# Seven-product pairs: the four sums are cast and split in two halves, and the products come in another order

## The chip, the core and the metric

The kernel runs on one core of a Trainium2 chip. The metric is the device time of one launch in microseconds (us). The engines are PE (TensorE, matmuls), DVE (VectorE), ACT (ScalarE), POOL (GpSimd) and SP (SyncE, which here only issues DMA transfers).

## The reference

A two-layer encoder trunk for 256 tokens of width 2048. Layer 0 mixes tokens by neighbourhood attention and a gated recurrence, layer 1 by a pooling mixer and grouped attention. Each mixer is followed by a SwiGLU block of hidden width 5632, which is where the change lies:

```python
def swiglu(x, w_gate, w_up, w_down):
    return (jax.nn.silu(x @ w_gate) * (x @ w_up)) @ w_down
...
for layer in range(DEPTH):
    ...
    x = layer_norm(DN_ALPHA * x + y, ln_mix_g[layer], ln_mix_b[layer])
    f = swiglu(x, ffn_w_gate[layer], ffn_w_up[layer], ffn_w_down[layer])
    x = layer_norm(DN_ALPHA * x + f, ln_ffn_g[layer], ln_ffn_b[layer])
```

All data are float32.

## The kernel before

**Precision.** PE multiplies in a rounded 32-bit format (`fp32r`). So each operand is kept as two parts: `hi`, a cast by ACT, and `lo`, the rest, by a subtraction on DVE. The helper `split` issues the two (L127, L128). A product of two such operands takes three matmuls (`mm3`, L292: hi·lo, hi·hi, lo·hi), each 128 x 128 by 128 x 512.

**SwiGLU.** The hidden width is cut in 11 chunks of 512 columns, and the chunks in three phases of 3, 4 and 4. A phase computes gate and up projection of its chunks and then multiplies them into the down projection. The first phase uses a plain form. In the second and third, one call of `unit` makes one chunk: so there are 4 units in a phase, 8 in a layer, 16 in all ("second unit" below is the second of a phase).

A unit runs over 8 pairs of 128-row weight blocks, for gate and up together. A pair is a 2 x 2 block product: two token tiles by gate and up. Most pairs are ordinary: weights come in two loads of 512 KB (`load_half`: tile `raw`, split into `whi` and `wlo`), and take 8 block products. The pairs 5, 6 and 7 (5 and 6 in the last unit of a phase, so 44 in all) are done with seven products (Strassen's scheme in Winograd's form). `load_seven` prepares their weights:

- one load of 1 MB into `rs` (one buffer, L443), which holds four 512-column blocks;
- the cast of the first three blocks on ACT (L444) and their `lo` part on DVE (L448), into entries 0 to 2 of `sh` and `sl`, which have two buffers and seven entries;
- four sums of blocks on DVE into `z` (one buffer): two in one instruction (L445), then one each (L446, L447);
- the split of the four sums into entries 3 to 6 of `sh` and `sl`: one 128 x 2048 cast (L127) and one 128 x 2048 subtraction (L128).

`forms` holds the matching sums of the token side, made once in a phase (tiles `fmh`, `fml`). `SEVEN_ORDER` (L453) names for each product the weight entry, the token form and the PSUM bank.

**Banks and the end of a unit.** The eight PSUM banks form two sides, `aside` and `bside`, four each. A unit gathers in c11, c21, c12, c22 on one side and in the special banks p1, p6, p5, p7 on the other. At its end DVE and ACT combine them (L485 to L499), and the sides change roles: the next unit's c banks are this unit's special banks. PE can begin a bank of the next unit when its last reader has run: p1 is read by L485, p6 by L486, p5 by L487 and L489, p7 by L488.

**What sets the order.** The kernel is written for a scheduler, which chooses the order of instructions on each engine by its own cost estimates and by priorities: the loads and splits of weights are written with priority 400, the end of a unit with 1000. So an edit in `load_seven` may move instructions anywhere in the units. DMAs of weights all go through SP's queue in the order of issue; a load waits for its buffer: `rs` until the last sum (L447) and L448 have read it, `raw` (four buffers) until its `wlo` subtraction has run.

Of the kernel before, what the change touches and what calls it, by code (L numbers as in the profile page):

```python
# [80 lines left out]
def trunk(ctx: ExitStack, tc: tile.TileContext, a, out):  # L81
# [44 lines left out]
    def split(hi, lo, src):  # L126
        nc.scalar.copy(hi, src)  # L127
        return nc.vector.tensor_tensor(lo, src, hi.bitcast(F32), op=sub).ins  # L128
# [304 lines left out]
    def load_seven(sp, src, behind):  # L433

        with ExitStack() as order:
            order.enter_context(tc.high_priority(offset=400))
            if behind:
                order.enter_context(tc.issue_after(behind))
            raw = sp.tile([P, 4, NCH], F32, tag="rs", name="rs", bufs=1)
            hi = sp.tile([P, 7, NCH], F32R, tag="sh", name="sh", bufs=2)  # L440
            lo = sp.tile([P, 7, NCH], F32R, tag="sl", name="sl", bufs=2)
            z = sp.tile([P, 4, NCH], F32, tag="z", name="z", bufs=1)
            last_load[0] = nc.sync.dma_start(raw, src).ins  # L443
            nc.scalar.copy(hi[:, :3], raw[:, :3])  # L444
            nc.vector.tensor_tensor(z[:, :2], raw[:, 0:3:2], raw[:, 3:4].to_broadcast([P, 2, NCH]), op=add)  # L445
            nc.vector.tensor_tensor(z[:, 2], z[:, 0], raw[:, 2], op=add)  # L446
            nc.vector.tensor_tensor(z[:, 3], z[:, 2], raw[:, 1], op=add)  # L447
            nc.vector.tensor_tensor(lo[:, :3], raw[:, :3], hi[:, :3].bitcast(F32), op=sub)  # L448
            split(hi[:, 3:], lo[:, 3:], z)
        return lambda i: (hi[:, i, :], lo[:, i, :])  # L450


    SEVEN_ORDER = ((0, "11", "p1"), (5, "f", "p6"), (3, "e", "p5"), (4, "g", "p7"), (1, "12", "c11"), (2, "h", "c12"), (6, "22", "c21"))  # L453

    def unit(sp, pairs, sevens, w, lhs, forms, yT, opening):

# [2 lines left out]
        left = {n: 4 * (len(pairs) - len(sevens)) // 2 for n in b}  # L459
        for _, _, n in SEVEN_ORDER:  # L460
            left[n] = left.get(n, 0) + len(sevens)

        def product(name, x, wt):
            left[name] -= 1
            mm3(b[name], x, wt, name not in begun, left[name] == 0)
            begun.add(name)

        behind = [low[-n] if opening and n else None for n in BEHIND]
        for p in pairs:
            if p in sevens:  # L470
                if "p1" not in b:
                    b.update((n, side_bank(True)) for n in ("p1", "p6", "p5", "p7"))
                wt = load_seven(sp, w[p], behind.pop(0))
                for i, x, name in SEVEN_ORDER:
                    product(name, forms[p][x], wt(i))
            else:
                for n, ks in ((0, (2 * p, 2 * p + 1)), (1, (2 * p + 1, 2 * p))):
                    hi, lo = load_half(w[p][:, 2 * n : 2 * n + 2])
                    for tok in range(NT):
                        for kk in range(2):  # L480
                            product(f"c{tok + 1}{n + 1}", lhs(tok, ks[kk]), (hi[:, kk, :], lo[:, kk, :]))
                    half_done()
# [658 lines left out]
def build(nc, arrays):  # L1141
    args = {}
    for name, v in arrays.items():
        t = nc.dram_tensor(name, v.shape, mybir.dt.from_np(v.dtype), kind="ExternalInput")
        args[name[3:]] = t.ap()
    out = nc.dram_tensor("out", (T, D), F32, kind="ExternalOutput").ap()
    with tile.TileContext(nc, schedule_with_timeline_sim=True) as tc:
        trunk(tc, args, out)
# [11 lines left out]
```

## Time and profile before

| | |
|---|---|
| median of 3 runs | 2190.99 us (2190.37 to 2191.4) |
| profiled execution: its own time | 2194.07 us |
| profiled execution: its span | 2192.3 us |
| granted PE clock | 0.998 |
| ACT busy | 1051.0 us, 48% |
| POOL busy | 52.1 us, 2% |
| read from memory | 416.78 MB, 191 GB/s over the span |

The profiled execution is one launch, recorded by the hardware; its span is the time from the first to the last recorded instruction, and its own time is a little above. A row of an engine's timeline has the start in us, the duration, the engine, the line, the operation, output and inputs by their names, and the shape; in brackets behind it the idle time before it and what ended that. In the view of DMA issues the last number is the time from issue to landing.

### The profile page before, as it was taken

Reading aid. Unit: us, or ns where it says so; the run is one execution under the profiler, and the core shown is the slowest. Engines: PE = TensorE matmul, PEld = TensorE weight load, DVE = VectorE, ACT = ScalarE, POOL = GpSimd, SP = SyncE. Lnnn points to the kernel's source line nnn. Section 1 sums busy time; section 2 is a strip of 40 time slices with the busy share of each in tenths; the row PEclk is TensorE's granted clock in tenths of the full one; section 3 lists DMA queues with packets and bytes.
Section 4 is the critical chain, followed back from the end, with each engine's and each line's share of the span. In section 5 each row is a group of like instructions: output and inputs, shape, how many; then the busy total and the mean of one; then the engine's idle time right before and its main releaser. Section 6 shows DMA issues by size and latency. Waiting matters only on the chain.

```text
span 2192.3 us, 26626 instructions
## 1 busy us (share of the span) xinstructions
PE 2172.9 (99%) x10048; PEld 1804.1 (82%) x10048; DVE 1558.2 (71%) x1954; ACT 1051.0 (48%) x1278; POOL 52.1 (2%) x51
## 2 busy tenths in 40 slices
PE   9999999999999999999999999999999999999997
PEld 7888888888888888888888888888888888888886
DVE  6886688567537787577876776666367896768865
ACT  6445544546425454444545554455344554445442
POOL 0000001000000000000000300000000000000000
PEclk9999999999999999999999999999999999999999
DMA  8555536684636555565548553747456555655573
GB/s 296 164 164 174 173 126 192 200 286 138 232 123 225 185 204 191 188 232 182 196 158 302 172 183 106 238 147 254 142 185 235 182 179 192 223 174 192 175 247 117
DMA packets 112850, 420.64 MB, mean 192 GB/s; under 512 B 13776, under 2 KB 16848, under 8 KB 105808
## 3 DMA queue, kind: packets, MB, share of 16 engines
q1 hardware_dynamic: 112720, 418.93, 57.5%
q8 instruction: 79, 1.29, 0.2%
q14 instruction: 51, 0.42, 0.1%
HBM read 416.78 MB, written 2.10 MB: 191 GB/s over the span
## 4 chain that ended last, share of the span: by engine, by line
PE 91%; DVE 4%; DMA 3%; issue 1%; ACT 1%; SPq 0%; DVEq 0%; ACTq 0%
PE acc L292 42%; PE bside L292 20%; PE aside L292 18%; PE mx L292 6%; DMA rs<-in_gu 2%; PE mx L729 1%; PE tr L124 1%; DVE wlo L128 1%; DMA raw<-in_gu 1%; DVE sl L448 1%; DVE sl L128 0%; PE mx L775 0%; PE aside L124 0%; PE bside L124 0%; PE mx L985 0%
## 5 line engine op out<-in xcount | busy, mean ns | idle before, releaser
L128 DVE TENSOR_TENSOR wlo<-raw,whi 128x1024 fp32r<-128x1024 f32 (+1 forms) x673 | 817.2, 1224 | 435.2 <-ACT whi L127 424.6
L127 ACT CAST whi<-raw 128x1024 fp32r<-128x1024 f32 (+1 forms) x673 | 703.9, 1052 | 817.5 <-PE acc L292 263.5
L292 PE MATMUL acc<-whi,xTl 128*128 128x512 f32 x864 | 342.8, 397 | 4.8 <-ACT whi L127 4.8
L292 PE MATMUL acc<-whi,xTh 128*128 128x512 f32 x864 | 339.8, 393 | 0.0
L292 PE MATMUL acc<-wlo,xTh 128*128 128x512 f32 x864 | 337.6, 393 | 0.1
L292 PE MATMUL acc<-whi,yTl 128*128 128x512 f32 x512 | 200.6, 392 | 0.1
L292 PE MATMUL acc<-whi,yTh 128*128 128x512 f32 x512 | 199.6, 390 | 0.0
L292 PE MATMUL acc<-wlo,yTh 128*128 128x512 f32 x512 | 197.7, 390 | 0.0
L292 PEld LDWEIGHTS acc<-whi,xTl 128*128 128x128 f32 x864 | 162.9, 189 | 37.0 <-ACT whi L127 5.5
L292 PEld LDWEIGHTS acc<-wlo,xTh 128*128 128x128 f32 x864 | 162.7, 188 | 33.6 <-DVE wlo L128 0.9
L292 PEld LDWEIGHTS acc<-whi,xTh 128*128 128x128 f32 x864 | 163.1, 189 | 31.1
L292 PE MATMUL aside<-whi,xTl 128*128 128x512 f32 x336 | 131.5, 391 | 0.4
L292 PE MATMUL bside<-whi,xTl 128*128 128x512 f32 x336 | 131.4, 391 | 0.3
L292 PE MATMUL aside<-whi,xTh 128*128 128x512 f32 x336 | 131.0, 390 | 0.0
L292 PE MATMUL bside<-whi,xTh 128*128 128x512 f32 x336 | 131.0, 390 | 0.0
L292 PE MATMUL bside<-wlo,xTh 128*128 128x512 f32 x336 | 128.1, 390 | 0.0
L292 PE MATMUL aside<-wlo,xTh 128*128 128x512 f32 x336 | 128.1, 390 | 0.0
L292 PEld LDWEIGHTS acc<-wlo,yTh 128*128 128x128 f32 x512 | 96.1, 188 | 20.5 <-DVE wlo L128 0.5
L292 PEld LDWEIGHTS acc<-whi,yTl 128*128 128x128 f32 x512 | 96.2, 188 | 19.7 <-DVE yTl L991 0.3
L292 PEld LDWEIGHTS acc<-whi,yTh 128*128 128x128 f32 x512 | 96.2, 188 | 19.4
L128 DVE TENSOR_TENSOR sl<-z,sh 128x2048 fp32r<-128x2048 f32 x44 | 100.7, 2289 | 6.7 <-ACT sh L127 6.1
L444 ACT CAST sh<-rs 128x1536 fp32r<-128x1536 f32 x44 | 65.3, 1483 | 76.3 <-DMA rs<-in_gu 35.8
(266 smaller groups left out, 3447.6 us busy)
## 6 DMA issues: line engine op xcount, KB each, us to landing
raw<-in_gu SPq DMA_DIRECT2D x264, 512.0 KB, 4.7
raw<-in_down SPq DMA_DIRECT2D x176, 512.0 KB, 3.9
raw<-in_ab_in SPq DMA_DIRECT2D x127, 512.0 KB, 4.2
rs<-in_gu SPq DMA_DIRECT2D x44, 1024.0 KB, 5.7
raw<-in_cd_in SPq DMA_DIRECT2D x40, 512.0 KB, 4.3
raw<-in_ab_out SPq DMA_DIRECT2D x32, 512.0 KB, 4.5
raw<-in_cd_out SPq DMA_DIRECT2D x32, 512.0 KB, 4.3
bias<-in_na_bias SPq DMA_DIRECT2D x32, 64.0 KB, 4.2
```

What stands on the lines that cost most here:

```text
L124: return nc.tensor.transpose(o, src, eye)
L127: nc.scalar.copy(hi, src)
L128: return nc.vector.tensor_tensor(lo, src, hi.bitcast(F32), op=sub).ins
L292: ins = nc.tensor.matmul(o, lhs[a], rhs[b], start=start and n == 0, stop=stop and n == 2)
L444: nc.scalar.copy(hi[:, :3], raw[:, :3])
L448: nc.vector.tensor_tensor(lo[:, :3], raw[:, :3], hi[:, :3].bitcast(F32), op=sub)
L729: nc.tensor.matmul(m[:, 2 * h + s, :], kk[:, h, s * P : (s + 1) * P], qq[:, h, r * P : (r + 1) * P], start=True, stop=True,)
```

## The change

In `load_seven` the split of the four sums is done in two halves: first the sums 0 and 1 (entries 3 and 4), then the sums 2 and 3 (entries 5 and 6). Each half is a 128 x 1024 cast and a 128 x 1024 subtraction. And in `SEVEN_ORDER` the products of the entries 3 and 4 now come ahead of that of entry 5.

```diff
@@ -446,11 +446,12 @@
             nc.vector.tensor_tensor(z[:, 2], z[:, 0], raw[:, 2], op=add)
             nc.vector.tensor_tensor(z[:, 3], z[:, 2], raw[:, 1], op=add)
             nc.vector.tensor_tensor(lo[:, :3], raw[:, :3], hi[:, :3].bitcast(F32), op=sub)
-            split(hi[:, 3:], lo[:, 3:], z)
+            for s in (slice(0, 2), slice(2, 4)):
+                split(hi[:, 3:][:, s], lo[:, 3:][:, s], z[:, s])
         return lambda i: (hi[:, i, :], lo[:, i, :])
 
 
-    SEVEN_ORDER = ((0, "11", "p1"), (5, "f", "p6"), (3, "e", "p5"), (4, "g", "p7"), (1, "12", "c11"), (2, "h", "c12"), (6, "22", "c21"))
+    SEVEN_ORDER = ((0, "11", "p1"), (3, "e", "p5"), (4, "g", "p7"), (5, "f", "p6"), (1, "12", "c11"), (2, "h", "c12"), (6, "22", "c21"))
```

There are 44 instructions more on ACT and 44 more on DVE; PE has the same number of matmuls. From L450 on, all line numbers of the new kernel are one higher: the first read of p6 is L486 before and L487 after. The scheduler also sets a different order within the second and third phases of both layers. Three places of it:

At the end of a second unit, DVE (`g` and `u` are the tiles of the unit's end, `sl` and `wlo` the `lo` parts of weights). Before:

```order
L445 TENSOR_TENSOR z<-rs 128x1024
L128 TENSOR_TENSOR wlo<-raw,whi 128x1024
L446 TENSOR_TENSOR z<-z,rs 128x512
L448 TENSOR_TENSOR sl<-rs,sh 128x1536
L447 TENSOR_TENSOR z<-z,rs 128x512
L128 TENSOR_TENSOR wlo<-raw,whi 128x1024
L486 TENSOR_TENSOR g_6585<-g_6584,bside 128x512
L487 TENSOR_TENSOR u_6586<-g_6585,bside 128x512
L490 TENSOR_TENSOR g_6584<-g_6584,aside 128x512
L128 TENSOR_TENSOR sl<-z,sh 128x2048
```

And after:

```order
L445 TENSOR_TENSOR z<-rs 128x1024
L128 TENSOR_TENSOR wlo<-raw,whi 128x1024
L446 TENSOR_TENSOR z<-z,rs 128x512
L448 TENSOR_TENSOR sl<-rs,sh 128x1536
L128 TENSOR_TENSOR sl<-z,sh 128x1024
L447 TENSOR_TENSOR z<-z,rs 128x512
L128 TENSOR_TENSOR wlo<-raw,whi 128x1024
L487 TENSOR_TENSOR g_6597<-g_6596,bside 128x512
L128 TENSOR_TENSOR sl<-z,sh 128x1024
L488 TENSOR_TENSOR u_6598<-g_6597,bside 128x512
```

The first half of the split has moved ahead of the last sum and of the first read of p6; the second half stands right behind that read, where the whole split came two instructions later.

At the end of a third unit, DVE. Before:

```order
L486 TENSOR_TENSOR g_6905<-g_6904,aside 128x512
L487 TENSOR_TENSOR u_6906<-g_6905,aside 128x512
L490 TENSOR_TENSOR g_6904<-g_6904,bside 128x512
L128 TENSOR_TENSOR sl<-z,sh 128x2048
L488 TENSOR_TENSOR g_6905<-g_6905,aside 128x512
L492 TENSOR_TENSOR u_6906<-bside,u_6906 128x512
L445 TENSOR_TENSOR z<-rs 128x1024
```

And after:

```order
L487 TENSOR_TENSOR g_6923<-g_6922,aside 128x512
L128 TENSOR_TENSOR sl<-z,sh 128x1024 x2
L488 TENSOR_TENSOR u_6924<-g_6923,aside 128x512
L491 TENSOR_TENSOR g_6922<-g_6922,bside 128x512
L445 TENSOR_TENSOR z<-rs 128x1024
L489 TENSOR_TENSOR g_6923<-g_6923,aside 128x512
```

Both halves come ahead of the reads of p5, and the first sums of the next pair (L445, which waits for that pair's load) ahead of the read of p7 (L489).

At the same place PE, just after the new unit's first seven-product pair. Before:

```order
L292 MATMUL aside_6924<-sh_7018,xTh1_3821 128x512
L292 MATMUL aside_6924<-sl_7019,xTh1_3821 128x512
L292 MATMUL aside_6925<-whi_6946,xTl0_3822 128x512
L292 MATMUL aside_6925<-whi_6946,xTh0_3820 128x512
L292 MATMUL aside_6925<-wlo_6947,xTh0_3820 128x512
```

And after, where `whi_7071` is a raw pair that comes later in the unit:

```order
L292 MATMUL aside_6942<-sh_7036,xTh1_3821 128x512
L292 MATMUL aside_6942<-sl_7037,xTh1_3821 128x512
L292 MATMUL aside_6941<-whi_7071,xTl0_3822 128x512
L292 MATMUL aside_6941<-whi_7071,xTh0_3820 128x512
L292 MATMUL aside_6942<-whi_7071,xTl1_3823 128x512
L292 MATMUL aside_6942<-whi_7071,xTh1_3821 128x512
L292 MATMUL aside_6943<-whi_6964,xTl0_3822 128x512
```

Four matmuls on the banks already open now come ahead of the next bank. Their weights are cast on ACT directly behind the cast of the next pair's `rs` load (L444).

## The prediction

> **What bounds the kernel now.** The first view is the page's own head, the busy time of each engine with its share of the span.
>
> ```profile
> PE 2172.9 (99%) x10048; PEld 1804.1 (82%) x10048; DVE 1558.2 (71%) x1954; ACT 1051.0 (48%) x1278; POOL 52.1 (2%) x51
> ```
>
> PE is busy for 99% of the span, and the diff leaves its work alone: the same products with the same shapes. So the change can only act through moments in which PE stands still or starts late. The waits of PE and the chain give how many there are and how fast PE goes when nothing holds it.
>
> ```profile
> PE acc L292 <- ACT whi L127: 4.8, 1, 4.8
> PE mx L292 <- DVE ptl L128: 1.2, 1, 1.2
> 734.44 2.72 PE aside L292 x12
> ```
>
> The two largest waits (total, times, longest) are 4.8 and 1.2 us, on the banks `acc` and `mx` of other stages. But 12 matmuls in 2.72 us are one per 0.227 us, and against that pace small losses can be read that the waits do not list. They lie at the end of a 512-column unit, where the four PSUM banks of the special products must be read by VectorE before the next unit's matmuls may overwrite them. PE at the end of the second unit of layer 0's second phase, and then of the third unit of layer 1's:
>
> ```profile
> 799.85 0.40 PE L292 MATMUL bside<-whi,xTl 128*128 128x512 f32 x1
> 802.80 0.39 PE L292 MATMUL bside<-sh,xTh 128*128 128x512 f32 x1
> 803.29 0.50 PE L292 MATMUL bside<-sl,xTh 128*128 128x512 f32 x1
> 803.89 0.50 PE L292 MATMUL bside<-whi,xTl 128*128 128x512 f32 x1
> 804.23 0.39 PE L292 MATMUL bside<-whi,xTh 128*128 128x512 f32 x1
> 1796.39 0.50 PE L292 MATMUL aside<-sl,xTh 128*128 128x512 f32 x1
> 1796.98 0.50 PE L292 MATMUL aside<-whi,xTl 128*128 128x512 f32 x1
> 1797.32 0.40 PE L292 MATMUL aside<-whi,xTh 128*128 128x512 f32 x1
> ```
>
> At 802.80 the next start is due 0.227 later, at 803.03, and comes at 803.29: 0.26 lost. The one after it is 0.37 late, the next 0.11: 0.74 us at this end. At 1796 it is 0.36 and 0.11: 0.47 us. Four units (the second of each of four phases) end like the first, two like the other, so all that shorter chains on VectorE could give back is 4 x 0.74 + 2 x 0.47 = 3.9 us, 0.18%. A measurement of this kernel tells about 0.2% from no change, 4.4 us, so the ceiling of the gain lies below what would count as faster.
>
> What those ends wait for is a VectorE chain that begins with the landing of an `rs` load and then runs without a hole. The chain of waits gives the load, VectorE's timeline the rest:
>
> ```profile
> 785.03 7.55 DMA rs<-in_gu
> 792.68 1.23 DVE L445 TENSOR_TENSOR z<-rs 128x1024 f32<-128x1024 f32 x1 [5.33 <-DMA rs<-in_gu]
> 793.83 1.22 DVE L128 TENSOR_TENSOR wlo<-raw,whi 128x1024 fp32r<-128x1024 f32 x1
> 794.96 0.68 DVE L446 TENSOR_TENSOR z<-z,rs 128x512 f32<-128x512 f32 x1
> 795.56 1.75 DVE L448 TENSOR_TENSOR sl<-rs,sh 128x1536 fp32r<-128x1536 f32 x1
> 797.23 0.68 DVE L447 TENSOR_TENSOR z<-z,rs 128x512 f32<-128x512 f32 x1
> 797.83 1.22 DVE L128 TENSOR_TENSOR wlo<-raw,whi 128x1024 fp32r<-128x1024 f32 x1
> 798.97 0.68 DVE L486 TENSOR_TENSOR g<-g,bside 128x512 f32<-128x512 f32 x1
> 799.75 0.69 DVE L487 TENSOR_TENSOR u<-g,bside 128x512 f32<-128x512 f32 x1
> 800.36 0.68 DVE L490 TENSOR_TENSOR g<-g,aside 128x512 f32<-128x512 f32 x1
> 800.95 2.28 DVE L128 TENSOR_TENSOR sl<-z,sh 128x2048 fp32r<-128x2048 f32 x1
> 803.16 0.68 DVE L488 TENSOR_TENSOR g<-g,bside 128x512 f32<-128x512 f32 x1
> ```
>
> From 792.68 to 803.84 VectorE has no free moment. L486 frees p6's bank, L488 the bank that PE takes at 803.89, and the large `sl` subtraction stands between them.
>
> **The split itself.** Prices from the costliest groups and from the tile view of `sh`:
>
> ```profile
> L128 DVE TENSOR_TENSOR sl<-z,sh 128x2048 fp32r<-128x2048 f32 x44 | 100.7, 2289 | 6.7 <-ACT sh L127 6.1
> L128 DVE TENSOR_TENSOR wlo<-raw,whi 128x1024 fp32r<-128x1024 f32 (+1 forms) x673 | 817.2, 1224 | 435.2 <-ACT whi L127 424.6
> L127 ACT CAST whi<-raw 128x1024 fp32r<-128x1024 f32 (+1 forms) x673 | 703.9, 1052 | 817.5 <-PE acc L292 263.5
> L127 ACT CAST sh<-z x44: 1907/1913/1921, 694.7 to 2066.0; 128x2048 fp32r<-128x2048 f32 x44
> ```
>
> A half has the shape of a `wlo` subtraction: 2 x 1.224 - 2.289 = +0.16 us busy per pair on VectorE, 44 times 7 us; on ScalarE 2 x 1.052 - 1.913 = +0.19, 8.4 us. In a back-to-back chain a 1024-wide one takes 1.14 from start to start (797.83 to 798.97) and the large one 2.21 (800.95 to 803.16), so the split lengthens a chain by 0.07 us. Nearly all of it lies beside PE, since VectorE is busy for 71% and ScalarE for 48%; where that cover is gone, at the six ends, the order on VectorE decides, below.
>
> The Trainium skill (VectorE: DVE Perf Modes, section "The DRAIN you can't avoid") says that the next instruction does not start until the pipe is empty. The rows here start each instruction some 0.08 us before the end of the one ahead, so by that rule each half would cost its whole 1.22 us in a chain, and the sum below would be 4 x 0.08 = 0.3 us higher; the rows decide.
>
> **Second units (four ends).** In the new order on VectorE the first `sl` half stands right behind L448 and ahead of L447, `wlo` and the first read of a special bank; the second half right behind that read. ScalarE's half is there by then: the first two sums are done at 793.9, and the cast takes 1.05. Nothing earlier in the chain moves, so with the start-to-start times of the rows: first half 797.23 to 798.37, L447 to 798.97, `wlo` to 800.11, then L486's work, whose end comes 0.68 later, and PE follows 0.06 behind (803.84 to 803.89): 800.85. PE wants that bank at 799.85. So 1.00 us is lost there, where nothing was lost. In exchange the second half and the other three reads end at about 803.9, and PE, now 15 matmuls later (15 x 0.227 = 3.41), reaches the next bank at 804.26 without a wait. Against 803.89 this is **+0.36 us** at each of four ends: one wait takes the place of two, and is longer. The new product order moves p6's product two places back within a pair, 6 matmuls or 1.4 us; the first read of p6 comes when VectorE gets to it, not when PE is done (PE was in the new unit's banks before 799.85), so that stays hidden, and neither costs nor gives.
>
> **Third units.** In layer 1 both halves come ahead of L487, and the sums of the *next* pair ahead of L488: one 1.14 for the sums more ahead of L488's release. PE's order there changes as well: behind the last product of the new unit's first seven-pair come four matmuls of a raw pair, whose cast stands on ScalarE behind the cast of the next `rs` load. The rows of layer 1, then of layer 0:
>
> ```profile
> 1795.91 1.48 ACT L444 CAST sh<-rs 128x1536 fp32r<-128x1536 f32 x1 [1.11 <-PE aside L292]
> 1797.29 1.99 ACT L127 CAST whi<-raw 128x1024 fp32r<-128x1024 f32 x2
> 844.51 0.68 DVE L488 TENSOR_TENSOR g<-g,aside 128x512 f32<-128x512 f32 x1
> 845.54 2.00 ACT L127 CAST whi<-raw 128x1024 fp32r<-128x1024 f32 x2
> 846.47 0.39 PE L292 MATMUL aside<-whi,xTl 128*128 128x512 f32 x1
> ```
>
> The first of the two casts ends at 1797.29 + 1.05 = 1798.34, so PE goes on at 1798.38 and not at 1796.98: **+1.40 us** in each phase of layer 1, in which the second unit's 0.36 is already contained (the chain hangs on a load's landing, not on PE). In layer 0 L488 has ended at 845.19, 1.28 us before PE asks; the cast ends at 846.59 and PE is there at 846.47: +0.1, beside the 0.36 of the second unit.
>
> First units and last units have 2 us and more between the last read and PE's need by the same reckoning, so the extra 0.07 and the moved half stay hidden. At a phase's opening one raw load falls behind an `rs` load on SP's queue; the raw load has about 3 us to spare, so nothing.
>
> Sum so far: 2 x (0.36 + 0.1) + 2 x 1.40 = **+3.7 us**.
>
> **The loads.** An `rs` load of 1 MB takes the longer, the shorter the time since the raw loads ahead of it were issued. Issues of SP, and the landing times:
>
> ```profile
> 824.55 2.12 SPq L168 DMA_DIRECT2D raw<-in_gu  x2
> 830.25 0.33 SPq L443 DMA_DIRECT2D rs<-in_gu  x1
> rs<-in_gu SPq DMA_DIRECT2D x1, 1024.0 KB, 4.7
> 1775.40 2.07 SPq L168 DMA_DIRECT2D raw<-in_gu  x2
> 1780.12 6.57 DMA rs<-in_gu
> 783.12 0.33 SPq L168 DMA_DIRECT2D raw<-in_gu  x1
> DMA to landing us min/median/max: 4.6/5.7/8.8
> ```
>
> The third row answers for the load of 830.25. With 3.58 us between the last raw issue's end and the `rs` issue it lands in 4.7; with 2.65 in 6.57; with 1.58 (783.45 to 785.03) in 7.55. Now the `rs` load after a second unit waits for L447, which the half ahead of it delays by 1.14, and VectorE's raw subtractions behind that pair's sums free their buffers some 0.7 to 1.3 later (an estimate from the same chain). The `rs` load of the third unit keeps its time, since PE releases its `sh` buffer. In layer 0 the gap falls from 3.58 to about 2.9 and the load grows by 1.4; in layer 1 from 2.65 to about 1.7 and it grows by 0.8. Both third-unit chains hang on that landing, so it counts in full once the slack is gone: 2 x 1.4 + 2 x 0.8 = 4.4, less some 0.8 where layer 0's unused wait absorbs it: **+3.6 us**. Bounds: nothing at all (the raw issues do not move), and the slowest landing, 8.8, at both layer 1 ends and 6.57 at both of layer 0: 2 x 2.2 + 2 x 1.9 = 8.2.
>
> The Trainium skill (DMA: Bandwidth & Descriptors, section "Queues, rings and completion order") says that each engine consumes a queue's descriptors in ring order; the three landings agree, since the later load waits out what is left of the earlier ones. By a queue without order the 3.6 would be zero.
>
> Total: 3.7 + 3.6 = +7.3 us on the profiled execution's 2194.07, 2201.4. The median of the runs stands 3.1 below that execution, so **2198 us** is forecast.
>
> **Rivals.**
> - *The loads keep their times* (raw issues are held by something other than VectorE): only +3.7, 2194.7, within 0.2%. For it: between 1.58 and 2.65 the landing changes by 1 us only. Against: the step to 4.7.
> - *Not slower: the early half shortens the chain.* If the `rs` load of the second units lands in 4.7 instead of 7.55, the whole chain begins 2.85 earlier, all six ends are free of waits, and the 3.9 us come back: 2187.1. It decides from a landing 1.0 us shorter on, since then the bank is read by 799.85. For it: with the first half written early, the `sl` buffer is complete sooner for PE. Against: that load is issued when L448 of the pair before is done, at 785.03, and no instruction ahead of that moves.
> - *No effect:* the added waits take the place of waits of the same size; within 1 us of 2191.
> - *Both layers meet the worst landings, and the next pair's sums block VectorE ahead of L488* until an `rs` load lands: 3.7 + 8.2 = +11.9, 2202.9.
>
> **How the numbers follow.** Forecast, with its own range of 2196 to 2201: 0.48. Loads as before, 2194.7: 0.25, of which a fifth lies past the 0.2% line of 2195.4. Chain shortened, 2187.1: 0.10, of which half passes the line of 2186.6. No effect: 0.06. Worst landings: 0.11. Slower: 0.48 + 0.05 + 0.11 = 0.64; same: 0.20 + 0.05 + 0.06 = 0.31; faster 0.05. The range from 2193 to 2203 leaves out the shortened chain and the case of no effect, 0.16.
>
> **What would show it.** PE's waits in the second units: one of about 1.0 us at the first bank of the new unit, with L487 (new numbering) as the releaser, and none later. Third units of layer 1: a gap of 1.6 us ahead of a matmul on `whi`, released by ScalarE's cast. The landing of the third units' `rs` loads: over 6 us in layer 0. VectorE busy 7 us more, ScalarE 8.4. The forecast is wrong if PE enters the new unit at 799.85 without a wait, or if the landings shrink.

## Result and the profile after

The changed kernel's median is 2197.91 us (2194.78 to 2202.66, 11 runs), that of the kernel before beside it 2192.51 (2190.37 to 2196.02): the ratio is 1.0022 with a 95% interval of 1.0014 to 1.0030, or +4.8 us (3.1 to 6.6); the two medians are 5.4 us apart. A later comparison, on another occasion, gave 1.0019 (1.0010 to 1.0028). So it is slower, as forecast in sign, and by two thirds of the forecast +7.3 us in size. The profiled execution took 2195.99 us, 1.9 more than that of before, so it shows less of the loss than the median does; why is the subject of what follows.

The page's head and PE's waits of the changed kernel (L numbers from L450 on are one higher than before):

```profile
span 2194.1 us, 26706 instructions
PE 2171.2 (99%) x10048; PEld 1803.8 (82%) x10048; DVE 1559.9 (71%) x1998; ACT 1054.7 (48%) x1322; POOL 55.5 (3%) x51
```

```profile
PE acc L292 <- ACT whi L127: 5.4, 3, 4.8
PE aside L292 <- ACT whi L127: 2.1, 1, 2.1
PE bside L292 <- ACT whi L127: 1.6, 1, 1.6
PE aside L292 <- DVE g L487: 0.6, 2, 0.4
PE bside L292 <- ACT g L486: 0.5, 1, 0.5
```

The second and third rows are new: PE waits, in the banks of the SwiGLU units, for a cast of ScalarE. Both lie at third units of layer 0. SP, ScalarE and PE at the first of them:

```profile
829.38 0.33 SPq L443 DMA_DIRECT2D rs<-in_gu  x1
840.44 0.33 SPq L443 DMA_DIRECT2D rs<-in_gu  x1
845.74 1.47 ACT L444 CAST sh<-rs 128x1536 fp32r<-128x1536 f32 x1 [4.27 <-PE aside L292]
847.12 1.04 ACT L127 CAST whi<-raw 128x1024 fp32r<-128x1024 f32 x1
845.76 0.39 PE L292 MATMUL aside<-sl,xTh 128*128 128x512 f32 x1
848.21 0.50 PE L292 MATMUL aside<-whi,xTl 128*128 128x512 f32 x1 [2.06 <-ACT whi L127]
```

PE is ready at 845.99 and starts at 848.21, 0.05 after the end of the cast of `whi`. That cast stands behind the cast of the next pair's `rs` load, which was issued at 840.44, landed at 845.36 and was cast from 845.74 on. (The bracket names PE for that wait. The instruction waits for a DMA and for a matmul that ended before 843; a wait for several is put down to the last event that the profile sees.) On ScalarE this cast stood behind that of the load before the change, too (844.16 and 845.54 in the profile of before). What is new is PE's order, which needs it ahead of the next bank. The load of 840.44 waits in its turn for the sums of the pair before it, whose load left at 829.38. So two loads in a row lie on the path, and the slower of the two is the first: 6.7 us, where the one before the change took 4.7.

In layer 1 the same place loses almost nothing, because there the first load landed in 5.0:

```profile
rs<-in_gu SPq DMA_DIRECT2D x1, 1024.0 KB, 5.0
1799.45 0.39 PE L292 MATMUL aside<-sl,xTh 128*128 128x512 f32 x1
1799.98 0.50 PE L292 MATMUL aside<-whi,xTl 128*128 128x512 f32 x1
```

That is 0.30 lost, and 0.37 before the change. Last, the second units. VectorE's chain, PE at the new unit's first bank, and the landing of the load that starts the chain:

```profile
rs<-in_gu SPq DMA_DIRECT2D x1, 1024.0 KB, 6.7
791.68 1.22 DVE L445 TENSOR_TENSOR z<-rs 128x1024 f32<-128x1024 f32 x1 [4.51 <-DMA rs<-in_gu]
796.23 1.22 DVE L128 TENSOR_TENSOR sl<-z,sh 128x1024 fp32r<-128x1024 f32 x1
797.36 0.69 DVE L447 TENSOR_TENSOR z<-z,rs 128x512 f32<-128x512 f32 x1
797.97 1.22 DVE L128 TENSOR_TENSOR wlo<-raw,whi 128x1024 fp32r<-128x1024 f32 x1
799.10 0.68 DVE L487 TENSOR_TENSOR g<-g,bside 128x512 f32<-128x512 f32 x1
799.50 0.39 PE L292 MATMUL bside<-sl,xTh 128*128 128x512 f32 x1
799.84 0.50 PE L292 MATMUL bside<-whi,xTl 128*128 128x512 f32 x1
```

The chain has the order and the spacing of the forecast (a half takes 1.13 from start to start), but it begins 1.0 earlier (L445 at 791.68 and not at 792.68): the load took 6.67 and not 7.55, and left 0.11 earlier. PE loses 0.11 at the first bank, where 1.00 was forecast.

Summed over all ends of units (start-to-start over 0.227 by more than 0.1, from PE's timeline), the profiled execution before loses 1.2 us in layer 0 and 2.9 in layer 1, the one after 5.9 and 1.2. This sum accounts for the spans of all kernels below: in all 14 profiles the span less the time that PE loses so in the units' banks is 2186.8 to 2188.9, while the spans run from 2186.8 to 2203.3. Three questions follow: is it the split or the order of products, is it layer 0 alone, and is it the cast behind the load.

### The profile page after: what moved, and what is told of

Its sections match the earlier page's. It is cut to its first block, busy times and chain, and to the rows that moved or that the text cites. A ratio compares the mean times of both kernels' runs of the same rounds, so it can differ in the third digit from the quotient of the medians.

```text
span 2194.1 us, 26706 instructions
## 1 busy us (share of the span) xinstructions
PE 2171.2 (99%) x10048; PEld 1803.8 (82%) x10048; DVE 1559.9 (71%) x1998; ACT 1054.7 (48%) x1322; POOL 55.5 (3%) x51
## 4 chain that ended last, share of the span: by engine, by line
PE 96%; DVE 2%; DMA 1%; issue 1%; ACT 0%; SPq 0%; DVEq 0%; ACTq 0%
PE acc L292 43%; PE bside L292 22%; PE aside L292 20%; PE mx L292 7%; PE mx L730 1%; PE tr L124 1%; DMA rs<-in_gu 1%; DVE wlo L128 0%; PE mx L776 0%; PE aside L124 0%; PE bside L124 0%; PE mx L986 0%; DVE sl L448 0%; DMA raw<-in_ab_in 0%; ACT whi L127 0%
## 5 line engine op out<-in xcount | busy, mean ns | idle before, releaser
L444 ACT CAST sh<-rs 128x1536 fp32r<-128x1536 f32 x44 | 65.3, 1484 | 114.0 <-DMA rs<-in_gu 64.8
L128 DVE TENSOR_TENSOR sl<-z,sh 128x1024 fp32r<-128x1024 f32 x88 | 105.6, 1218 | 0.0
```

## The experiments

**1. The split alone and the order of products alone.** `split_only` has the first hunk of the diff, `order_only` the second.

> Only the split in halves, the old order of products. Theory A (the order of instructions that the two halves lead to is the cause: in layer 0 PE stands 2.2 and 1.7 us at the end of the third units for a raw pair's cast behind the next pair's load): PE's and ACT's order are those of the changed kernel, so the ratio to before is 1.0015 to 1.003, and the profile shows the two stalls. Theory C (the order of products is the cause, p6 finished later): within 0.1% of before, no such stall.

> Only the new order of products, the split in one piece. Theory A: the instructions stand as before but for the products themselves; ratio 0.9995 to 1.0005, ends of the units lose what they lost before (0.74 us at the second units). Theory C: 1.0015 to 1.003.

Measured: `split_only` 1.0045 (1.0033 to 1.0058), `order_only` 1.0001 (0.9992 to 1.0010). The order of products alone does nothing; the loss comes with the split. PE's waits of `split_only`, then its third unit in layer 1:

```profile
PE aside L292 <- ACT whi L127: 3.4, 2, 2.2
PE bside L292 <- ACT whi L127: 3.3, 2, 1.7
1801.82 0.39 PE L292 MATMUL aside<-sl,xTh 128*128 128x512 f32 x1
1803.41 0.50 PE L292 MATMUL aside<-whi,xTl 128*128 128x512 f32 x1 [1.20 <-ACT whi L127]
```

Here all four third units wait for the cast, those of layer 1 too: 1.36 us at 1803.41, where the prediction had 1.40. In this execution the four loads ahead of them landed in 7.4, 7.5, 6.2 and 7.4.

The 1.0045 lies above the expected range and is about twice the changed kernel's loss. ScalarE's and SP's instructions stand in the same order in both kernels, and VectorE's differ by one `wlo` in a phase. Whether the new order of products halves the loss once the split is in, or the loads came later on this occasion and chip (the changed kernel was not run beside it), is not separated. The next two runs, from the same occasion and with both hunks, speak for the second: their losses add up to 0.41%.

The profile of `order_only`, which but for the products and four places on VectorE at the ends of last units has the instruction order of before, shows no lost time at all at the ends of units (0.1 us; its span is 2186.9):

```profile
PE acc L292 <- ACT whi L127: 4.9, 2, 4.7
802.81 0.39 PE L292 MATMUL bside<-sl,xTh 128*128 128x512 f32 x1
803.12 0.50 PE L292 MATMUL bside<-whi,xTl 128*128 128x512 f32 x1
```

Its loads at the second units landed in 7.1, 6.6, 6.8 and 6.5, in before's profile in 7.6, 7.4, 7.4 and 8.0, at the same distance (1.59 us) from the raw loads ahead. So the same load at the same place and distance takes 6.3 to 8.0 us from one execution to the next, and the 3.9 us that the prediction read off the profile of before were those of an execution with slow loads.

**2. One layer at a time.** `layer0` and `layer1` have both hunks for the units of one layer only. The split in `layer0` (the order of products is chosen in the same way):

```diff
+            if layer_now[0] == 0:
+                for s in (slice(0, 2), slice(2, 4)):
+                    split(hi[:, 3:][:, s], lo[:, 3:][:, s], z[:, s])
+            else:
+                split(hi[:, 3:], lo[:, 3:], z)
```

> The change in layer 0 alone. Theory A: all of the loss is here. Ends of layer 0's units lose 5.7 us by the changed kernel's profile against 1.5 before: +4.2 us, ratio 1.0015 to 1.003. Theory B (the prediction's: both layers lose alike, 1.85 us in a phase of layer 0 and 2.2 in a phase of layer 1): +3.7, ratio 1.0017. The two differ in the next run.

> The change in layer 1 alone. Theory A: ends of layer 1's units lose 1.2 us against 2.6 before: -1.4 us, ratio 0.9988 to 1.0000. Theory B: two phases of +2.2 us, ratio 1.002.

Measured: `layer0` 1.0023 (1.0015 to 1.0032), `layer1` 1.0018 (1.0009 to 1.0027). Both layers lose, and nearly alike, as the prediction had it. That the two add up to twice the loss of the whole change, measured on other occasions, stays unexplained but for the scatter of the loads. What I had read from the one profile after the change, a gain in layer 1, was wrong: it was an execution with fast loads there. The profile of `layer1` shows the named wait:

```profile
1795.82 0.50 PE L292 MATMUL aside<-whi,xTl 128*128 128x512 f32 x1 [1.31 <-ACT whi L127]
```

**3. The cast ahead of the load's cast, the sums behind the read of p7, and the first half behind the last sum.** Three kernels that each change one place of the new order, run with the changed kernel once more.

> The changed kernel once more, beside the next three. Theory A (third units: PE waits for a raw pair's cast that stands on ScalarE behind the cast of the next pair's load; how long depends on when that load lands in this execution): ratio 1.002 to 1.0045, stalls of 1 to 2.4 us at some of the four third units, 0 to 0.8 at the second units. Theory B (the prediction's +0.36 at each second unit as well): 0.36 more at each second unit than before has.

It gave 1.0019 (1.0010 to 1.0028), just below the expected range. Its profiled execution, the fastest of its eleven, has no stall of 1 us: the third units lose 0.46, 0, 0.91 and 0.45, with first loads that landed in 4.8, 4.7, 5.6 and 5.1, and the second units 0.15 to 0.38.

`cast_first` swaps two casts on ScalarE in the last unit of a phase, so that the cast of pair 6's load is issued behind the first cast of the raw pair (`cast_behind`; the lines that set it are left out here):

```diff
-            nc.scalar.copy(hi[:, :3], raw[:, :3])
+            with ExitStack() as late:
+                if cast_behind[0]:
+                    late.enter_context(tc.issue_after(cast_behind[0]))
+                nc.scalar.copy(hi[:, :3], raw[:, :3])
```

> The changed kernel, but in the last unit of a phase the cast of the raw pair is issued on ScalarE ahead of the cast of the second seven-product pair's load instead of behind it; everything up to there stands as in the changed kernel. Theory A: the stalls of 1.4 to 2.4 us at the third units fall to 0.2 to 0.6 (then the read of p7, which stands behind the next pair's sums, is late); the ratio to before falls to 0.9995 to 1.0015. Rival D (VectorE's chain is what ends last there, not the cast): stalls and ratio stay as in the changed kernel, 1.002 or more.

Measured 1.0001 (0.9992 to 1.0009), beside the 1.0019 of the changed kernel on the same occasion: the loss is gone. ScalarE and PE at the third unit of layer 0, and PE at the third unit of the phase after it (line numbers are shifted by the edit: L451 is the load's cast, L497 the read of p7):

```profile
845.13 1.05 ACT L129 CAST whi<-raw 128x1024 fp32r<-128x1024 f32 x1 [4.45 <-PE aside L294]
846.09 1.48 ACT L451 CAST sh<-rs 128x1536 fp32r<-128x1536 f32 x1
846.65 0.39 PE L294 MATMUL aside<-sl,xTh 128*128 128x512 f32 x1
846.88 0.39 PE L294 MATMUL aside<-whi,xTl 128*128 128x512 f32 x1
1106.74 0.50 PE L294 MATMUL bside<-whi,xTl 128*128 128x512 f32 x1 [0.30 <-DVE g L497]
```

The cast ends at 846.18, PE goes on at 846.88 without a pause. At 1106.74 the load ahead had landed in 7.2 us, and PE loses 0.46 for the read of p7: this is the remainder that was expected. The two third units of layer 1, with first loads of 6.8 and 7.1, lose 0.45 and 0.44 there, where landings of 6.2 and more cost 1.4 to 2.4 in the order of the changed kernel. So it is the cast, and not a faster load, that made the difference.

`sum_late` holds VectorE's first sums of a unit's second seven-product pair behind the read of p7; the scheduler then also gives PE its old order at this place (next bank first, the raw pair later):

```diff
-            nc.vector.tensor_tensor(z[:, :2], raw[:, 0:3:2], ...)
+            with ExitStack() as late:
+                if sevens_done[0] == 1 and p7_read[0]:
+                    late.enter_context(tc.issue_after(p7_read[0]))
+                nc.vector.tensor_tensor(z[:, :2], raw[:, 0:3:2], ...)
```

> The changed kernel, but VectorE's first sums of a unit's second seven-product pair are issued behind the read of p7, as they were before the change; with that PE's order at the third units is the old one (next bank first, raw pair later). Theory A: stalls at the third units 0.5 us at most; ratio 0.998 to 1.0005. Theory B: the second units still lose 0.36 each more than before: 1.0005 to 1.0015. Rival E (the split itself, 88 more instructions, costs): 1.002.

Measured 0.9998 (0.9989 to 1.0007). All 88 added instructions are in this kernel, so the split itself costs nothing that can be measured. Its third units of layer 0 had late first loads (6.9 and 7.0), and PE lost at most 0.35 at any bank there. The largest that remains is at the second units, in the read of p6 (L495 there):

```profile
PE aside L292 <- DVE g L495: 0.7, 2, 0.5
PE bside L292 <- DVE g L495: 0.6, 2, 0.4
```

`half_late` issues both halves behind the last sum (L447):

```diff
-            for s in (slice(0, 2), slice(2, 4)):
-                split(...)
+            with tc.issue_after(z3):
+                for s in (slice(0, 2), slice(2, 4)):
+                    split(...)
```

> The changed kernel with both halves issued on VectorE behind the last sum (L447), so that the first half no longer stands ahead of it. By the order of PE at the third units (next bank first, as before) theory A gives no stall for the cast there: ratio 0.998 to 1.001. Theory B (the first half ahead of the sum delays the chain): the read of p6 at the second units comes 1.1 us earlier than in the changed kernel. Rival E: 1.002.

Measured 1.0063 (1.0050 to 1.0076), above every ratio that was expected. The second units lose nothing now, as theory B said, but the loads also changed there: they left 2.4 us behind the raw loads and not 1.6, and landed in 4.6 to 4.8. The loss is a new one at the third units. PE's waits, and ScalarE there:

```profile
PE aside L292 <- ACT g L487: 5.3, 2, 2.9
PE bside L292 <- ACT g L487: 3.1, 2, 2.4
838.19 1.48 ACT L444 CAST sh<-rs 128x1536 fp32r<-128x1536 f32 x1 [5.11 <-DMA rs<-in_gu]
839.58 1.04 ACT L127 CAST sh<-z 128x1024 fp32r<-128x1024 f32 x1
840.52 1.04 ACT L127 CAST whi<-raw 128x1024 fp32r<-128x1024 f32 x1
841.46 0.58 ACT L487 COPY g<-aside 128x512 f32<-128x512 f32 x1
```

The copy of p1 (L487 here), which frees the new unit's first bank, stands behind a half of the cast, a raw cast and the cast of a load that took 7.0. This kernel changed too much to isolate its question; it shows the same mechanism at another bank.

**4. The loads from another queue.** In the next four kernels only the engine that issues the `rs` loads is another than in the kernel before, in `sum_late` or in the changed kernel: `nc.gpsimd.dma_start` or `nc.scalar.dma_start` in place of `nc.sync.dma_start`. The scheduler moves other instructions with it.

> The kernel before, with the 1 MB rs loads issued by GpSimd instead of SP, so that they stand in no queue behind raw loads. Theory F (a load is slow because it stands in line behind raw loads of its own queue): the loads ahead of the second units land in 4.7 to 5.5 us instead of 6.5 to 8, no stall at the unit ends, ratio 0.998 to 0.9995. Rival G (what counts is the bytes in flight on the shared DMA engines, in whatever queue): they land in 6.5 us or more, ratio 0.9995 to 1.001 or, with a slower issue, above.

> The kernel before, with the rs loads issued by ScalarE. Same theories for the landing. On ScalarE the issue also stands in line with the casts, so loads that need no buffer wait may start later; ratio by F 0.998 to 1.001, by G 1.000 to 1.003.

> The changed kernel with VectorE's sums behind the read of p7 and the rs loads issued by GpSimd. By F no stall at the ends of the units is left: the second units' 0.35 to 0.6 us and the third units' 0.2 go, about 3 us, ratio 0.998 to 0.9995. By G 1.000, as without the move to GpSimd.

> The changed kernel as it is, with the rs loads issued by GpSimd. If the loss of the changed kernel is the landing time of the third units' loads, met by less slack (theory A with F), it shrinks with the landing: stalls at the third units 0 to 0.6 us, ratio to before 0.999 to 1.0005. If the order of the casts alone is enough (theory A without F), 1.0015 to 1.003 as in the changed kernel.

Measured: `pool_before` 0.9993 (0.9984 to 1.0002), `actq_before` 1.0051 (1.0038 to 1.0063), `pool_sum_late` 0.9990 (0.9981 to 0.9999), `pool_after` 0.9995 (0.9986 to 1.0004). The load of the second unit in `pool_before`, issued at nearly the same time as in before:

```profile
785.32 0.54 POOL L443 DMA_DIRECT2D rs<-in_gu  x1 [15.37 <-DVE sl L448]
rs<-in_gu POOLq DMA_DIRECT2D x1, 1024.0 KB, 5.0
```

Of the 24 loads issued at the ends of second and third units (the first at each) in the three kernels with GpSimd, 23 land in 4.9 to 5.3 us and one in 6.9; on SP's queue those of the second units took 6.3 to 8.0, but for `half_late`. In `pool_after` the loss is gone, too (0.1 us lost at the ends), but not by the landings alone: with them the scheduler moved ScalarE's instructions, and the raw pair's casts now come ahead of the cast of the second load:

```profile
844.91 1.04 ACT L127 CAST whi<-raw 128x1024 fp32r<-128x1024 f32 x1
847.09 1.48 ACT L444 CAST sh<-rs 128x1536 fp32r<-128x1536 f32 x1 [1.14 <-DMA rs<-in_gu]
```

So this kernel has both repairs in one. That the loss needs both, the new order and a late load, is shown by the 16 third units that have the changed order in the profiles of the changed kernel (twice), `split_only`, `layer0` and `layer1`. The nine whose first load (of the two in a row) took 6.2 us or more lose 1.36 to 2.39 at the wait for the cast, the one with 5.6 loses 0.91, and the six with 5.1 or less lose 0 to 0.46.

Whether it is the queue of its own that makes GpSimd's loads fast, or the raw loads of SP, which run further ahead (the last one leaves 2.7 us before this load and not 1.6), is not separated by these runs. In `half_late` a distance of 2.4 us was enough for 4.6 to 4.8 on SP's queue, so the queue may not be needed.

`actq_before` lies above both of its expected ranges. PE waits 1.7 to 3.7 us at the third units, each time for L485, the copy of p1 on ScalarE, which now also issues the loads; what delays that copy stays open.

`pool_sum_late` has the lowest ratio of the kernels, and its profile loses nothing at the ends: 2190.05 us beside 2191.78 for before, 0.10% with an interval that ends just below 1 and overlaps those of `pool_before` and `pool_after`.

## Why the prediction came out as it did

- **The bound and the ceiling.** Right. Executions in which no end of a unit waits (`order_only`, `pool_sum_late`) have spans of 2186.9 and 2186.8 us; before's has 2192.3 with 4.1 us lost, where the prediction had 3.9. The ends were less alike than it took them (0.74, 0.48, 0.48 and 1.15 at the four second units).
- **The split's price.** Right that it is hidden: `sum_late` carries it at 0.9998. VectorE's busy time grew by 1.7 us and ScalarE's by 3.7, though, and not by 7 and 8.4. By the Trainium skill (VectorE: DVE Perf Modes, section "The DRAIN you can't avoid") the next instruction waits until the pipe is empty, but one that is not "held" starts earlier. The half at 796.23 ends at 797.45 and the next starts at 797.36, so the rows are of the second kind, which the prediction left out.
- **Second units, +0.36 each.** The mechanism is right, the size wrong. The forecast 1.00 us at a landing of 7.55 means a wait of the landing less 6.55. In the changed kernel's profile the four loads took 6.7, 7.1, 6.4 and 6.9, and the bank came 0.11, 0.58, 0 and 0.34 late; in the second profile of it 6.9, 6.7, 6.7 and 6.9 gave 0.38, 0.15, 0.18 and 0.33. The prediction's own sign of being wrong here, PE entering the new unit without a wait, shows at one of these eight ends. The step that failed is the base: I took one execution's 7.55 for the load's duration, and it was the slow end of 6.3 to 8.0.
- **Third units.** Right in the mechanism that was named: a raw pair's cast behind the next pair's load. Of layer 1's 1.40 the first profile shows 0.30 (landing 5.0), `split_only` 1.36 (landing 6.2) and `layer1` 1.47 (6.3). For layer 0 I had let a part be absorbed by slack; it lost 2.2 and 1.7 in the profile, and 0.5 and 0 in the second one. Rival D, by which VectorE's chain ends last there, is refuted by `cast_first`. One wait was left out: the prediction has VectorE read all four special banks, but p1 is read by ScalarE (L486), whose copy stands behind the cast of the same load. At six of the nine third units with the late loads PE lost 0.55 to 1.16 us more there.
- **The loads, +3.6.** Half right. In layer 0 the gap to the raw loads was 2.88 and 2.94 (forecast 2.9) and the landings 6.7 and 7.3 (forecast 6.1). In layer 1 I expected a gap of 1.7 and a landing of 7.4; the gap was 3.35 and the landing 5.0 and 4.8; this is the prediction's other sign of being wrong, landings that shrink. The mechanism holds even so. In every profile with the split (`half_late` aside, SP's queue), the gap was 9.2 less the landing of the load before, and at most 3.36; without the split it was 10.3 less that landing, and at most 3.58, with one exception among twelve. So the change takes 1.0 us of the gap, and a late load makes the next one leave closer behind its raw loads. The 1.7 was right for a load before of 7.6 us, as in the profile of before; here it took 4.95 and 5.69. Between gaps of about 2 and 3 us the landings of the third units' loads scatter from 4.7 to 7.8 over the profiles, so the straight line through three rows was too much to ask of them; at 3.58 seven of seven took 4.6 to 4.8, at 1.3 to 1.6 all loads of second and third units on SP's queue took 6.3 or more.
- **The sum.** +7.3 was forecast against +4.8 (3.1 to 6.6). The second units, +1.4 in the sum, gave about nothing, and layer 1's loads grew in some executions only. The measured change is nearer to the +3.7 of the rival in which the loads keep their times, though the loads did change; +7.3 lies outside the interval. So it is luck in part that the predicted 2198 us meets 2197.91 so closely: the kernel before had a median 1.5 us higher in the comparison than in its first three runs.

## To carry to other kernels

A chain that begins with a load has the load's scatter as its own: judge a change by the slack that it leaves for a late landing, not by the one landing that a profile happens to show, and look at several executions before saying which layer or place loses. When a scheduler may move instructions, splitting one of them can cost nothing by itself and still let a consumer be issued behind a transfer that it doesn't need; look for what now stands behind a waiting instruction on an in-order engine. The cheap repair was an order edge at that one place, and not the undoing of the split. And where each load waits for work on the one before, a late landing is passed on.

## What was not expected of the hardware

After a long wait PE may go on at half its clock. A stall is counted here as above, against 0.227 us from start to start. `split_only`, stretches around the 2.39 us stall of 846.9 to 849.3; in each row the times of the stretch, its length, the busy times of PE, its weight loads, VectorE, ScalarE and GpSimd, then the granted PE clock, the DMA share and GB/s:

```profile
846.00:849.00 3.00, 1.07 (x5) 0.56 (x3) 3.00 (x5) 2.17 (x2) 0.00 (x0) 1.00 0.40 154
849.00:851.00 2.00, 1.70 (x7) 1.37 (x8) 2.00 (x3) 2.00 (x4) 0.00 (x0) 0.93 0.03 8
851.00:854.00 3.00, 3.00 (x9) 2.33 (x8) 3.00 (x5) 0.67 (x1) 0.00 (x0) 0.50 0.11 30
854.00:860.00 6.00, 6.00 (x28) 4.98 (x27) 5.13 (x7) 2.38 (x3) 0.00 (x0) 0.99 0.62 210
```

PE starts again at full pace and drops to a clock of 0.50, here some 1.5 us later (0.4 to 1.5 in the others), for eight matmuls at 0.427 us from start to start: 8 x 0.2 = 1.6 us on top of the stall. In the SwiGLU units of these profiles no stall of up to 1.82 us was followed by it, of six from 2.05 to 2.61 us four were (2.05, 2.14, 2.39 and 2.51, but not the 2.22 of the changed kernel and the 2.61 of `half_late`), and both above 3 us were. The Trainium skill (TensorE: Matmul & The Clock Gate, section "Part 1: The HAM clock gate (the "warmup" mystery)") gives about 3.4 us of idling for the return to half rate; here shorter stalls sufficed. This makes late loads dearer than their lateness, in the executions in which a stall reaches two microseconds.
